# Turning an attention head's softmax weights by VectorE's blocks and a trip through DRAM in place of TensorE, in the second layer's mixer B

## The chip, the cores and the metric

One core of one Trainium2 chip runs the whole program. The metric is device time in microseconds (us), the median of three runs of the kernel before: 2664.96 us, lowest 2664.18, highest 2666.12. The names of the engines in the profile: PE is TensorE (PEld its weight loads), DVE is VectorE, ACT is ScalarE, POOL is GpSimd, SP is SyncE, which here only issues DMAs (SPq is its queue).

## The reference

The model is an encoder trunk of two layers on 256 tokens with 2048 channels. Each layer has a parallel mixer and a gated, convolved feed-forward part. Cut to what the change touches:

```python
h = rmsnorm(x, norm_mix[l]) * (1.0 + sc_a) + sh_a
qa, ka, va, qb, kb, vb, ga, gb = split_cols(h @ w_in[l])
...
ya = window_attention(qa, ka, va, sink_a[l]) @ w_proj_a[l]          # mixer A, 8 heads
...
yb = neighbourhood_attention(qb, kb, vb, rel_bias_b[l]) @ w_proj_b[l]  # mixer B, 8 heads
merged = jax.nn.sigmoid(ga) * ya + jax.nn.sigmoid(gb) * yb
x = x + gt_a * (merged @ w_out[l])
```

A head of mixer B is attention of 256 queries over 256 keys, each of 128 elements, with a learned bias and a mask on the scores: `p = softmax(q k^T * scale + bias)`, then `o = p v`. All of it is float32.

## The kernel before

**Weights.** All weight matrices are cut into 128x128 blocks and streamed from DRAM in the order in which they are used. Sixteen blocks are a unit (1 MB, tile `w`, pool `raw` with four buffers). A unit is loaded by SP (L286) and split in two halves: ScalarE copies a half into a rounded float32r part (L297) and VectorE computes the remainder (L298). Each half is a tile `hl`, of which there are four buffers, so that two units can be ready at once. A product is three matmuls a block (L314, L315, L316): high by high, high by low, low by high. The modulation weights (`aw`, L225) use the same four `raw` buffers, and VectorE reduces each of them in one long instruction (L226).

**What sets the order.** The tensor program is written out in the order of the weight stream. After each unit `Stream.tick` runs `bg.tick()`: first what was deferred to this tick, then each background job by its rate, a number of steps a tick. Attention is such a job: a step moves every live head one step on and may launch one more. In the second layer it runs at 0.4 steps a unit (`ATT[1]`) until mixer A's projection is done, and from then on, beside gate B, at `ATT_B[1]` = 0.21. Gate B has 16 units. At its end `bg.finish(job)` runs whatever steps are left, and mixer B's projection follows. Each engine works through its own queue in order; a planner that simulates the engines places instructions in these queues, so that one engine's instruction can stand ahead of its place in the program.

**A head of mixer B** (`head_b`, then `attend`) loads its bias into the tile `p` (L825) and splits q and k into halves at launch. Its steps then are:

1. scores on TensorE (L607), bias and row maximum on VectorE (L610), exponential and sums on ScalarE (L618), reciprocal on VectorE (L624), scaling on ScalarE (L626);
2. four 128x128 transposes on TensorE into one PSUM tile `tp` (L631), then the split of `tp` into `pT`, a rounded part on ScalarE (L389) and a remainder on VectorE (L390), then the split of v;
3. the product of v and `pT` on TensorE (L639) and its split into `oA` or `oB` (L641, L642).

The transposes are needed because the scores lie with queries across partitions, while the product wants keys there. `p` has two buffers, `pT` one. q and k of a pack of four heads lie in a tile (`packs[1]`, `packs[2]`); after launch their place in it is not read again.

Of the kernel before, what the change touches and what calls it, by code (L numbers as in the profile page):

```python
# [9 lines left out]
F32 = mybir.dt.float32  # L10
F32R = mybir.dt.float32r
AF = mybir.ActivationFunctionType
ALU = mybir.AluOpType
AX = mybir.AxisListType

P = 128
L = 2
D = 2048
S = 256
# [7 lines left out]
EPS = 1e-6  # L27
NEG = -1e30
SCALE = HEAD ** -0.5
GRID_W, NA_KH, NA_KW = 64, 8, 16  # L30


QKV_GROUPS = [1024, 0, 512, 2560, 3584, 1536, 3072, 4096, 2048]
# [45 lines left out]
H_RATE = [2.7, 1.7]  # L79

ATT = [1.288, 0.4]
ATT_B = [0.21, 0.21]

SCORES_3 = (1,)

ADA_ORDER = [[p * KC + k for k in range(KC) for p in ps] for ps in ((0, 1), (2,), (3, 4), (5,))]
ADA_ORDER = [i for part in ADA_ORDER for i in part]
# [47 lines left out]
def encoder(ctx: ExitStack, tc: tile.TileContext, a: dict, out: bass.AP):  # L135
    nc = tc.nc
    pool = lambda name, bufs, **kw: ctx.enter_context(tc.tile_pool(name=name, bufs=bufs, **kw))
# [12 lines left out]
    ev = pool("ev", 3)  # L150
    at = pool("at", 2)
    sm = pool("sm", 3)
    mm = pool("mm", 4, space=bass.MemoryType.PSUM)
    ax = pool("ax", 3, space=bass.MemoryType.PSUM)

    ident = const.tile([P, P], F32, name="ident")
    make_identity(nc, ident[:])
# [11 lines left out]
    def load(src, shape, name, p=const, **kw):  # L169
        t = p.tile(shape, F32, name=name, **kw)  # L170
        nc.sync.dma_start(t[:], src)
        return t
# [103 lines left out]
                pass  # L276

    bg = Paced()

    def unit_steps(l, u, by_halves=False):  # L280

        raw = rawp.tile([P, UB * P], F32, name=f"w{l}_{u}", tag="raw")
        if not by_halves:
            nc.sync.dma_start(raw[:], a["ws"][l, u])  # L286
        halves = []
        streamed = any(m == "w_in" and mo < GATE_A // P for m, _, mo in STREAMS[l][u * UB : (u + 1) * UB])
        at = OFF if streamed else 0
        for j in range(2):  # L290
            n = UB * P // 2
            hl = hlp.tile([P, 2 * n + ROW], F32R, name=f"hl{l}_{u}_{j}", tag="hl")
            hl = hl[:, at : at + 2 * n].rearrange("p (a n) -> p a n", a=2)
            r = raw[:, j * n : (j + 1) * n]
            if by_halves:
                nc.sync.dma_start(r, a["ws"][l, u][:, j * n : (j + 1) * n])
            nc.scalar.copy(hl[:, 0], r)  # L297
            nc.vector.tensor_tensor(out=hl[:, 1], in0=r, in1=hl[:, 0].bitcast(F32), op=ALU.subtract)  # L298
            halves.append(hl)
            if j == 0:  # L300
                yield halves
# [84 lines left out]
    def split(dst, src, scale=None):  # L386

        if scale is None:
            nc.scalar.copy(dst[:, 0], src)  # L389
            nc.vector.tensor_tensor(out=dst[:, 1], in0=src, in1=dst[:, 0].bitcast(F32), op=ALU.subtract)  # L390
            return
        nc.scalar.activation(out=dst[:, 0], in_=src, func=AF.Copy, scale=scale)
        nc.vector.scalar_tensor_tensor(
            out=dst[:, 1], in0=src, scalar=scale, in1=dst[:, 0].bitcast(F32), op0=ALU.mult, op1=ALU.subtract
        )
# [202 lines left out]
    def by(x):  # L598

        return ((0, 0), (0, 1), (1, 0))[: 2 * len(x) - 1]  # L600

    def attend(q, k, v, p, mask, scale, sink, o):

        sc = ax.tile([P, 2, S], F32, name="sc", tag="ax")
        for t in range(2):
            for i, j in by(q):
                nc.tensor.matmul(sc[:, t], q[i][:, t * P : (t + 1) * P], k[j], start=i + j == 0, stop=(i, j) == by(q)[-1])  # L607
        m = sm.tile([P, 2], F32, name="m", tag="m")
        for t in range(2):
            nc.vector.tensor_tensor_reduce(  # L610
                out=p[:, t], in0=sc[:, t], in1=mask[:, t], scale=scale, scalar=-3.0e38 if sink is None else sink,
                op0=ALU.add, op1=ALU.max, accum_out=m[:, t : t + 1],
            )
        nm = sm.tile([P, 2], F32, name="nm", tag="nm")
        nc.vector.tensor_scalar(out=nm[:], in0=m[:], scalar1=-1.0, scalar2=None, op0=ALU.mult)
        den = sm.tile([P, 2], F32, name="den", tag="den")
        for t in range(2):
            nc.scalar.activation(out=p[:, t], in_=p[:, t], func=AF.Exp, bias=nm[:, t : t + 1], accum_out=den[:, t : t + 1])  # L618
        if sink is not None:
            es = sm.tile([P, 2], F32, name="es", tag="es")  # L620
            nc.scalar.activation(out=es[:], in_=nm[:], func=AF.Exp, bias=sink)
            nc.vector.tensor_tensor(out=den[:], in0=den[:], in1=es[:], op=ALU.add)
        ri = sm.tile([P, 2], F32, name="ri", tag="ri")
        nc.vector.reciprocal(out=ri[:], in_=den[:])  # L624
        for t in range(2):
            nc.scalar.activation(out=p[:, t], in_=p[:, t], func=AF.Copy, scale=ri[:, t : t + 1])  # L626
        yield
        tp = ax.tile([P, 2, S], F32, name="tp", tag="ax")
        for k in range(2):
            for t in range(2):  # L630
                nc.tensor.transpose(tp[:, k, t * P : (t + 1) * P], p[:, t, k * P : (k + 1) * P], ident[:])  # L631
        pT = at.tile([P, 2, 2, S], F32R, name="pT", tag="pT", bufs=1)
        split(pT, tp[:])
        v = v()
        yield
        po = ax.tile([P, 512], F32, name="po", tag="ax")
        for i, j in by(v):
            for b in range(2):
                nc.tensor.matmul(po[:, :S], v[i][:, b], pT[:, j, b], start=i + j + b == 0, stop=i + b == 2)  # L639
        o = o()  # L640
        nc.scalar.copy(o[:, 0], po[:, :S])  # L641
        nc.vector.tensor_tensor(out=o[:, 1], in0=po[:, :S], in1=o[:, 0].bitcast(F32), op=ALU.subtract)  # L642
# [91 lines left out]
    tables = []  # L734

    def small(l):
# [7 lines left out]
        cw = load(a["cw"][l], [P, 2 * FC, 4], f"cw{l}", lay, tag="cw", bufs=1)  # L744
        nc.vector.tensor_scalar(out=gains[:, 2:3], in0=gains[:, 2:3], scalar1=SCALE, scalar2=None, op0=ALU.mult)
        rots = []
# [11 lines left out]
    for l in range(L):  # L758
# [35 lines left out]
        kTa, qTa = packs[0][:, 0:3:2], packs[0][:, 4:12]  # L794
# [3 lines left out]
        oA, oB = [], []  # L798

        def head_a(i):  # L800
            g = i // (HA // GA)
            if i >= 6:
                oA.append(paired(F32R, f"oA{l}_{i}"))
            elif i % 2 == 0:
                o = place(("y0", "y1", "y2")[i // 2], 4, F32R, f"oA{l}_{i}")
                oA.extend((o[:, :2], o[:, 2:]))
            q = in_halves(qTa[:, i], f"qA{l}_{i}", "qh", l in SCORES_3)
            if i % (HA // GA) == 0:
                kvs[0] = in_halves(kTa[:, g], f"kA{l}_{g}", "kh", l in SCORES_3)
            k = kvs[0]  # L810
            yield
            p = at.tile([P, 2, S], F32, name="p", tag="p")

            def v():
                if i % (HA // GA) == 0:
                    kvs[1] = in_halves(packs[0][:, 1:4:2, g * HEAD : (g + 1) * HEAD], f"vA{l}_{g}", "vh", True)
                return kvs[1]

            yield from attend(q, k, v, p, tables[0], SCALE, sink[:, i : i + 1], lambda: oA[i])

        def head_b(hb):
            b, i = packs[1 + hb // 4], hb % 4
            v = b[:, 4:8].rearrange("p (t a) s -> p t (a s)", t=2)
            p = at.tile([P, 2, S], F32, name="p", tag="p")
            nc.sync.dma_start(p[:], a["bias"][l, hb])  # L825
            q = in_halves(b[:, 8 + i], f"qB{l}_{hb}", "qh", l in SCORES_3)
            k = in_halves(b[:, i], f"kB{l}_{hb}", "kh", l in SCORES_3)
            yield
            yield from attend(
                q, k, lambda: in_halves(v[:, :, i * HEAD : (i + 1) * HEAD], f"vB{l}_{hb}", "vh", True), p, p, 1.0, None,  # L830
                lambda: oB_of(hb),
            )

        def oB_of(hb):
            if hb == 0:
                o = place("a", 12, F32R, f"oB{l}_{hb}")
                oB.extend(o[:, 2 * i : 2 * i + 2] for i in range(6))
            elif hb == 6:
                oB.extend(chunks_of(sp, "b0", 6, f"oB{l}_{hb}", 2))
            return oB[hb]  # L840
# [30 lines left out]
        for pi, (groups, gates) in enumerate(parts):  # L871
            last = pi == len(parts) - 1
            for g, part in enumerate(groups):
                have_h(part)
                pss = st.tokens(h, part)
                if pi == max(0, len(parts) - 2) and g == 0:
                    gains, sink, cw, rots = small(l)
                dst = packs[g // 3][:, 4 * (g % 3) : 4 * (g % 3) + 4]
                rows = dst.rearrange("p (t a) s -> p t (a s)", t=2)
# [54 lines left out]
        if l:  # L934
            bg.pace(job, ATT_B[l])
        gb = []
        for tag in ("y0", "y1", "y2"):
            t = place(tag, 4, F32, f"gb{l}_{tag}")
            gb += [t[:, i] for i in range(4)]
        for i in range(2):  # L940
            t = paired(F32, f"gb{l}_{i}")
# [56 lines left out]
        for gi, chunks in enumerate(FF_GROUPS):  # L998
# [34 lines left out]
            for cs in sets:  # L1033
                fns = [lambda p, e=e, c=c: e(p, c) for c in cs for e in (g_evac, v_evac)]
                src = bare.chunks if gi == 0 and cs[0] < BARE[1] // 2 else bare.h
# [113 lines left out]
```

## Time and profile before

| | |
|---|---|
| median of three runs | 2664.96 us (2664.18 to 2666.12) |
| span of the profiled execution, first to last instruction | 2663.2 us; the page gives no other time of that execution |
| instructions | 50845 |
| data read from DRAM, written to it | 695.03 MB, 2.10 MB |
| tile `tp`: transposes (L631) | 128, from 281.1 us to 1796.0 us, both layers and both mixers |
| second layer, attention | 1440 to 1802 us; mixer B's products (L639) from 1663.4 to 1802.2 us |
| second layer, mixer A's projection, gate B, mixer B's projection | about 1657 to 1708, 1708 to 1801, 1801 to 1847 us |

The page shows busy times and shares of the span for each engine, then the chain of work that ended last, followed back from the last instruction, then groups of instructions by source line. In a group, the numbers behind the first bar are the busy time in us and the mean of one in ns, and behind the second the idle time of that engine just before these instructions and what ended it. In a timeline, a row is the start, the duration, the engine, the line, the operation and the tiles, with a count. Matmuls are pipelined and their ends are modelled, so the start-to-start time is the one to read.

### The profile page before, as it was taken

The numbers are of one execution on the slowest core, as the hardware profiler recorded it, in microseconds if no ns is written. First come the engines' busy times: TensorE is split into PE (matmuls) and PEld (weight loads), VectorE is DVE, ScalarE is ACT, GpSimd is POOL, SyncE is SP. The second block draws the span as 40 slices with busy tenths as digits, with TensorE's granted clock in tenths as the row PEclk, the third lists the DMA queues.
The fourth block names the chain that finished last, engine by engine and source line by source line (L and its number), as shares of the span: only waits on it lengthen the run. The fifth ranks groups of instructions, "written<-read, shape, count | busy, mean of one in ns | idle before, by whom it ended". The sixth has DMA issues, their size and how long they took to land.

```text
span 2663.2 us, 50845 instructions
## 1 busy us (share of the span) xinstructions
PE 2650.9 (100%) x21256; PEld 2565.7 (96%) x21256; DVE 2102.2 (79%) x2959; ACT 1412.8 (53%) x2284; POOL 36.2 (1%) x25
## 2 busy tenths in 40 slices
PE   9999999999999999999999999999999999999999
PEld 7888899999999999999998889999999999999999
DVE  8898998997987888788976667768888866655664
ACT  5445865456644555355555566554565445544553
POOL 0001100000000000000000000000000000000000
PEclk9999999999999999999999999999999999999999
DMA  9987789885787878788766666666747765555554
GB/s 372 351 327 292 262 300 352 317 320 199 291 294 287 302 288 295 289 294 289 290 217 254 228 229 231 245 252 253 285 173 288 297 256 190 190 194 194 197 191 143
DMA packets 102039, 700.41 MB, mean 263 GB/s; under 512 B 12721, under 2 KB 15025, under 8 KB 17969
## 3 DMA queue, kind: packets, MB, share of 16 engines
q1 hardware_dynamic: 101810, 697.17, 71.4%
q8 instruction: 166, 2.72, 0.4%
q14 instruction: 63, 0.52, 0.1%
HBM read 695.03 MB, written 2.10 MB: 262 GB/s over the span
## 4 chain that ended last, share of the span: by engine, by line
PE 89%; DVE 6%; ACT 1%; issue 1%; DMA 1%; POOL 0%; SPq 0%; DVEq 0%; ACTq 0%
PE ps L314 25%; PE ps L316 25%; PE ps L315 25%; PE ps_t L377 4%; PE ps_t L379 4%; PE ps_t L378 4%; DVE hl L298 2%; DVE aw L226 2%; DMA aw<-in_aw 1%; PE sc L607 1%; PE po L639 1%; ACT hl L297 1%; PE tp L631 1%; POOL qrs L441 0%; PE qtp L580 0%
## 5 line engine op out<-in xcount | busy, mean ns | idle before, releaser
L298 DVE TENSOR_TENSOR hl<-w,hl 128x1024 fp32r<-128x1024 f32 x928 | 1128.3, 1222 | 360.0 <-ACT hl L297 357.6
L297 ACT CAST hl<-w 128x1024 fp32r<-128x1024 f32 x928 | 970.7, 1049 | 748.5 <-PE ps L316 518.1
L314 PE MATMUL ps<-h,hl 128*128 128x256 f32 x3328 | 922.8, 277 | 1.3 <-DVE ya L915 0.6
L315 PE MATMUL ps<-h,hl 128*128 128x256 f32 x3328 | 919.8, 276 | 0.0
L316 PE MATMUL ps<-h,hl 128*128 128x256 f32 x3328 | 919.8, 277 | 0.0
L314 PEld LDWEIGHTS ps<-h,hl 128*128 128x128 f32 x3328 | 624.8, 188 | 2.4 <-DVE ya L915 0.8
L315 PEld LDWEIGHTS ps<-h,hl 128*128 128x128 f32 x3328 | 625.3, 188 | 0.4 <-DVE h L470 0.2
L316 PEld LDWEIGHTS ps<-h,hl 128*128 128x128 f32 x3328 | 624.4, 188 | 0.0
L226 DVE CUSTOM_DVE_ANT_0 aw<-aw,cact,ab 128x2048 f32<-128x2048 f32 x189 | 443.5, 2347 | 48.8 <-DMA aw<-in_aw 47.8
L377 PE MATMUL ps_t<-hl,h 128*128 128x512 f32 x576 | 223.1, 392 | 2.6 <-ACT h L469 2.1
L378 PE MATMUL ps_t<-hl,h 128*128 128x512 f32 x576 | 224.9, 391 | 0.3
L379 PE MATMUL ps_t<-hl,h 128*128 128x512 f32 x576 | 224.3, 390 | 0.0
L994 DVE SCALAR_TENSOR_TENSOR u<-ps,cw,u 128x255 f32<-128x255 f32 x304 | 146.1, 481 | 66.5 <-ACT u L992 62.2
L992 ACT ACTIVATE u<-ps,cw 128x256 f32<-128x256 f32 x152 | 85.9, 565 | 187.9 <-PE ps L316 187.5
L316 PE MATMUL ps<-merged,hl 128*128 128x256 f32 x512 | 141.8, 277 | 0.4 <-DVE hl L298 0.4
L315 PE MATMUL ps<-merged,hl 128*128 128x256 f32 x512 | 141.6, 277 | 0.0
L314 PE MATMUL ps<-merged,hl 128*128 128x256 f32 x512 | 141.6, 277 | 0.0
L315 PE MATMUL ps<-act_o,hl 128*128 128x256 f32 x512 | 141.4, 276 | 0.0
L316 PE MATMUL ps<-act_o,hl 128*128 128x256 f32 x512 | 141.3, 276 | 0.0
L314 PE MATMUL ps<-act_o,hl 128*128 128x256 f32 x512 | 141.2, 276 | 0.0
L377 PEld LDWEIGHTS ps_t<-hl,h 128*128 128x128 f32 x576 | 107.9, 188 | 26.1 <-ACT h L469 3.1
L378 PEld LDWEIGHTS ps_t<-hl,h 128*128 128x128 f32 x576 | 108.1, 188 | 23.7 <-DVE hl L298 1.9
(231 smaller groups left out, 4612.5 us busy)
## 6 DMA issues: line engine op xcount, KB each, us to landing
w<-in_ws SPq DMA_DIRECT2D x463, 1024.0 KB, 4.9
aw<-in_aw SPq DMA_DIRECT2D x189, 1024.0 KB, 6.1
p<-in_bias SPq DMA_DIRECT2D x16, 256.0 KB, 4.2
x<-in_xT SPq DMA_DIRECT2D x4, 512.0 KB, 5.3
aw_o<-in_aw SPq DMA_DIRECT2D x2, 1024.0 KB, 12.3
out<-x SPq DMA_DIRECT2D x16, 128.0 KB, 2.1
w<-in_ws SPq DMA_DIRECT2D x2, 512.0 KB, 11.7
aw_b<-in_aw SPq DMA_DIRECT2D x1, 1024.0 KB, 18.1
```

Of the source, the lines that this page charges most:

```text
L226: nc.vector.tensor_tensor_reduce(out=raw[:], in0=raw[:], in1=cact[:], scale=1.0, scalar=ab[:, i : i + 1], op0=ALU.mult, op1=ALU.add, accum ...
L297: nc.scalar.copy(hl[:, 0], r)
L298: nc.vector.tensor_tensor(out=hl[:, 1], in0=r, in1=hl[:, 0].bitcast(F32), op=ALU.subtract)
L314: nc.tensor.matmul(out, hi, act[0], start=first, stop=False)
L315: nc.tensor.matmul(ps[:, :S], hi, act[1], start=False, stop=False)
L316: nc.tensor.matmul(out, lo, act[0], start=False, stop=last)
L377: nc.tensor.matmul(ps[:], xh, hi, start=kc == kcs[0], stop=False)
L378: nc.tensor.matmul(ps[:], xh, lo, start=False, stop=False)
L379: nc.tensor.matmul(ps[:], xl, hi, start=False, stop=kc == kcs[-1])
L607: nc.tensor.matmul(sc[:, t], q[i][:, t * P : (t + 1) * P], k[j], start=i + j == 0, stop=(i, j) == by(q)[-1])
L992: nc.scalar.activation(out=u, in_=ps, func=AF.Identity, scale=w[:, 1:2], bias=w[:, 3:4])
L994: nc.vector.scalar_tensor_tensor(out=u[:, to], in0=ps[:, of], scalar=w[:, j : j + 1], in1=u[:, to], op0=ALU.mult, op1=ALU.add)
```

## The change

In the second layer, all eight heads of mixer B (`MOVED[1] = (0, 8)`) no longer use TensorE's transposes. VectorE turns the two 128x256 halves of `p` in blocks of 32x32 into the room that q and k of the head occupied. For each of these, GpSimd's queue issues four DMAs of 32 KB, which carry the blocks to a DRAM tile at the place where the whole transpose wants them, in pieces of 128 bytes. SP's queue reads the two transposed halves back, 128 KB each, four ticks later (`BACK[1] = 4`), or in the head's step two steps on if that comes first. A manual dependency makes each read wait also for the newest unit's second weight split on VectorE (`halved`). `pT` is then split from these two SBUF rows, one after the other, in place of from PSUM. A head has two steps more. `ATT_B[1]` goes from 0.21 to 0.4. The first layer and mixer A keep TensorE's transposes (`MOVED` has zeros there).

```diff
-ATT_B = [0.21, 0.21]
+ATT_B = [0.21, 0.4]
...
+BACK = [3, 4]
+MOVED = [(0, 0), (0, 8)]
...
+    dram = pool("dram", 2, space=bass.MemoryType.DRAM)
...
+    def read_back(dst, src):
+
+        tc.add_manual_dep(nc.sync.dma_start(dst, src).ins, halved[0], BEHIND)
+
+    def later(n, fn):
+
+        if n == 0:
+            fn()
+        else:
+            bg.defer(lambda: later(n - 1, fn))
+
+    def turned_blocks(p, rows, n, tag):
+
+        y = dram.tile([P, n, S], F32, name=tag, tag=tag)
+        to = y[:].rearrange("(b i) n (t a j) -> t a i n b j", i=BLOCK, t=2, a=P // BLOCK)
+        for t, row in enumerate(rows):
+            nc.vector.transpose(out=row, in_=p[t])
+            src = row.rearrange("p (n b j) -> p n b j", n=n, j=BLOCK)
+            for a in range(P // BLOCK):
+                nc.gpsimd.dma_start(to[t, a], src[a * BLOCK : (a + 1) * BLOCK])
+        return y
...
-            nc.vector.tensor_tensor(out=hl[:, 1], in0=r, in1=hl[:, 0].bitcast(F32), op=ALU.subtract)
+            halved[0] = nc.vector.tensor_tensor(
+                out=hl[:, 1], in0=r, in1=hl[:, 0].bitcast(F32), op=ALU.subtract
+            ).ins.name
...
-        tp = ax.tile([P, 2, S], F32, name="tp", tag="ax")
-        for k in range(2):
-            for t in range(2):
-                nc.tensor.transpose(tp[:, k, t * P : (t + 1) * P], p[:, t, k * P : (k + 1) * P], ident[:])
-        pT = at.tile([P, 2, 2, S], F32R, name="pT", tag="pT", bufs=1)
-        split(pT, tp[:])
+        if rows is not None:
+            rows = rows()
+            y = turned_blocks([p[:, t] for t in range(2)], rows, 2, "pY")
+
+            def back():
+                for k in range(2):
+                    read_back(rows[k], y[:, k])
+
+            back = once(back)
+            later(BACK[sink is None], back)
+            yield
+            yield
+            back()
+            pT = at.tile([P, 2, 2, S], F32R, name="pT", tag="pT", bufs=1)
+            for k in range(2):
+                split(pT[:, :, k], rows[k])
+        else:
...
-                lambda: oB_of(hb),
+                lambda: oB_of(hb), (lambda: [b[:, 8 + i], b[:, i]]) if hb < MOVED[l][1] else None,
```

`once(fn)` calls `fn` the first time only.

More of the change, by code (lines that the diff above doesn't have):

```diff
@@ L29 @@
 SCALE = HEAD ** -0.5
+BEHIND = mybir.DependencyInfo(mybir.DependencyClass.Sync, mybir.DependencyReason.DATA)
 GRID_W, NA_KH, NA_KW = 64, 8, 16
+BLOCK = 32
 QKV_GROUPS = [1024, 0, 512, 2560, 3584, 1536, 3072, 4096, 2048]
@@ L278, in encoder, with once, run @@
     bg = Paced()
+    halved = [None]
+    def once(fn):
+        due = [fn]
+        def run():
+            if due:
+                due.pop()()
+        return run
+    def read_back(dst, src):
[14 more added lines that the diff above has]
+        return y
     def unit_steps(l, u, by_halves=False):
@@ L600, in by, with attend @@
         return ((0, 0), (0, 1), (1, 0))[: 2 * len(x) - 1]
-    def attend(q, k, v, p, mask, scale, sink, o):
+    def attend(q, k, v, p, mask, scale, sink, o, rows=None):
         sc = ax.tile([P, 2, S], F32, name="sc", tag="ax")
@@ L627, in attend @@
         yield
-        tp = ax.tile([P, 2, S], F32, name="tp", tag="ax")
-        for k in range(2):
-            for t in range(2):
-                nc.tensor.transpose(tp[:, k, t * P : (t + 1) * P], p[:, t, k * P : (k + 1) * P], ident[:])
-        pT = at.tile([P, 2, 2, S], F32R, name="pT", tag="pT", bufs=1)
-        split(pT, tp[:])
+        if rows is not None:
[13 more added lines that the diff above has]
+        else:
+            tp = ax.tile([P, 2, S], F32, name="tp", tag="ax")
+            for k in range(2):
+                for t in range(2):
+                    nc.tensor.transpose(tp[:, k, t * P : (t + 1) * P], p[:, t, k * P : (k + 1) * P], ident[:])
+            pT = at.tile([P, 2, 2, S], F32R, name="pT", tag="pT", bufs=1)
+            split(pT, tp[:])
         v = v()
@@ L817, in v, with rows @@
                 return kvs[1]
-            yield from attend(q, k, v, p, tables[0], SCALE, sink[:, i : i + 1], lambda: oA[i])
+            def rows():
+                spare = ev.tile([P, S], F32, name=f"spare{l}_{i}", tag="r", bufs=2)
+                return [qTa[:, i], spare[:]]
+            yield from attend(
+                q, k, v, p, tables[0], SCALE, sink[:, i : i + 1], lambda: oA[i], rows if i < MOVED[l][0] else None
+            )
         def head_b(hb):
```

## The prediction

> **What bounds the kernel now.** I read the page first: busy times, then the chain that ended last.
>
> ```profile
> span 2663.2 us, 50845 instructions
> PE 2650.9 (100%) x21256; PEld 2565.7 (96%) x21256; DVE 2102.2 (79%) x2959; ACT 1412.8 (53%) x2284; POOL 36.2 (1%) x25
> PE 89%; DVE 6%; ACT 1%; issue 1%; DMA 1%; POOL 0%; SPq 0%; DVEq 0%; ACTq 0%
> ```
>
> TensorE is busy for all but 12 us of the span and carries 89% of the chain; GpSimd is nearly empty. So the change is worth what it takes from TensorE's queue, less what it makes TensorE wait. An average can hide a stage with another limit, so I next asked for the busy time in the two stages in which mixer B of the second layer runs: the projection of mixer A (1657 to 1708 us) and gate B (1708 to 1801 us).
>
> ```profile
> core 0: us, PE busy (x) PEld busy (x) DVE busy (x) ACT busy (x) POOL busy (x), PEclk, DMA share, GB/s
> 1657.00:1708.00 51.00, 51.00 (x447) 51.00 (x446) 40.79 (x73) 27.73 (x51) 0.00 (x0) 1.00 0.69 252
> 1708.00:1801.00 93.00, 93.00 (x820) 93.00 (x819) 59.45 (x82) 48.71 (x84) 0.00 (x0) 1.00 0.67 246
> ```
>
> TensorE has no gap there, at a granted clock of 1.00. VectorE has 10 of 51 us and 34 of 93 us free, the DMA engines a third. Hence nothing can be gained here but TensorE instructions that disappear, and much can be added elsewhere before it shows. The waits of this stage say how far ahead the others are:
>
> ```profile
> L298 DVE TENSOR_TENSOR hl<-w,hl 128x1024 fp32r<-128x1024 f32 x53 | 64.7, 1224 | 44.8 <-ACT hl L297 44.8
> L297 ACT CAST hl<-w 128x1024 fp32r<-128x1024 f32 x54 | 56.7, 1050 | 45.8 <-PE ps L316 45.8
> L226 DVE CUSTOM_DVE_ANT_0 aw<-aw,cact,ab 128x2048 f32<-128x2048 f32 x9 | 21.1, 2348 | 1.0 <-DMA aw<-in_aw 0.9
> ```
>
> Groups of 1640 to 1800 us. ScalarE's weight copies wait for TensorE to free a buffer, and VectorE waits for ScalarE: both are paced by TensorE. No weight copy waits for a DMA.
>
> **What is removed: 32 transposes on TensorE.** Busy time overlaps between matmuls (each row says 0.28 us), so I take start-to-start times in TensorE's timeline.
>
> ```profile
> 1763.72 0.28 PE L316 MATMUL ps<-h,hl 128*128 128x256 f32 x1
> ...
> 1765.77 0.28 PE L316 MATMUL ps<-h,hl 128*128 128x256 f32 x1
> 1765.88 0.85 PE L639 MATMUL po<-pT,vB 128*128 128x256 f32 x6
> 1766.56 0.60 PE L631 MATMUL tp<-ident,p 128*128 128x128 f32 x4
> 1766.92 0.94 PE L607 MATMUL sc<-kB,qB 128*128 128x256 f32 x6
> 1767.70 0.28 PE L314 MATMUL ps<-h,hl 128*128 128x256 f32 x1
> ```
>
> From 1763.72 to 1765.77 lie 18 intervals (six turns of L314, L315, L316): 2.05 / 18 = 0.114 us a matmul. From 1765.77 to 1767.70 are 1.93 us with 12 wide matmuls and the closing interval in them: 13 x 0.114 = 1.48. The rest, 0.45 us, is what four transposes cost (0.11 each, not the 0.27 of a busy row).
>
> ```profile
> L631 PE MATMUL tp<-ident,p x32: 270/272/273, 1646.0 to 1796.0; 128*128 128x128 f32 x32
> L389 ACT CAST pT<-tp x8: 587/598/604, 1646.9 to 1796.7; 128x512 fp32r<-128x512 f32 x8
> L390 DVE TENSOR_TENSOR pT<-tp,pT x8: 679/681/683, 1648.3 to 1798.0; 128x512 fp32r<-128x512 f32 x8
> ```
>
> That tile's instructions from 1640 to 1800 us: 32 transposes, so eight groups of four. **8 x 0.45 = 3.6 us off TensorE.**
>
> **What the quicker pace moves.** With 0.21 steps a unit in gate B the last head isn't done when the stage ends; its last step is run there, and the first merge waits for it:
>
> ```profile
> 1804.66 0.40 PE L314 MATMUL ps<-oB,hl 128*128 128x256 f32 x2
> 1805.36 0.38 PE L315 MATMUL ps<-oB,hl 128*128 128x256 f32 x1 [0.30 <-DVE oB L642]
> ```
>
> The second of the two starts at 1804.78, the next at 1805.36: 0.58 less one interval, 0.47 us lost. At 0.4 a head needs two steps more, but 16 units give six steps (0.4 x 16 = 6.4). The head launched last, one step before the stage, needs five more steps and ends about a unit before the stage does. **0.5 us gained.** If I miscounted a step, the last read back and its splits run bare at that point: 4.2 us to land, as a bias load (row below), and 1.7 for the splits, some 6 us, once.
>
> **What is added on VectorE and ScalarE.** A head gets two block transposes of 128x256 and, in place of one split of 128x512 out of PSUM, two splits of 128x256 out of SBUF. The nearest rows are the splits of v, also 128x256 from SBUF:
>
> ```profile
> L389 ACT CAST vB<-packB 128x256 fp32r<-128x256 f32 x8 | 3.4, 421 | 0.0
> L390 DVE TENSOR_TENSOR vB<-packB,vB 128x256 fp32r<-128x256 f32 x8 | 3.3, 415 | 0.0
> ```
>
> No block transpose is in this trace. Its bounds are nothing and the 0.68 us of the 128x512 row; I take 0.42, the row with as many elements. VectorE: 2 x 0.42 + 2 x 0.42 - 0.68 = 1.0 us a head, 8 us in all; with about four heads in the projection stage it goes from 40.8 to 44.8 of 51 us. ScalarE: 2 x 0.42 - 0.60 = 0.24 us a head. On the path: nothing, hidden by the free time above. Without that cover it would be 8 us.
>
> **What is added on the queues.** GpSimd issues 8 writes of 32 KB a head, 64 in all; SP issues 16 reads of 128 KB, in the queue that also loads weights (w), modulation weights (aw) and bias. Per head 0.26 MB go out and come back, 4.2 MB in about 150 us: 28 GB/s beside 246. Hidden by the third of DMA time that is free.
>
> A read back waits for all eight writes, and what is queued behind it on SP are the loads of w and aw, on which VectorE and then TensorE wait. So its cover matters. The unit is 48 x 0.114 = 5.46 us.
>
> ```profile
> 1703.31 0.90 ACT L626 ACTIVATE p<-p,ri 128x256 f32<-128x256 f32 x2
> ```
> ```profile
> 1708.32 0.60 PE L631 MATMUL tp<-ident,p 128*128 128x128 f32 x4
> ```
>
> Head by head, p is ready at 1704.2, 4.1 us before its turn at the end of a unit, so VectorE can turn it that early. The read back also waits for the second half of the newest unit's weights:
>
> ```profile
> 1754.61 1.22 DVE L298 TENSOR_TENSOR hl<-w,hl 128x1024 fp32r<-128x1024 f32 x1
> 1758.98 1.23 DVE L298 TENSOR_TENSOR hl<-w,hl 128x1024 fp32r<-128x1024 f32 x1 [1.25 <-ACT hl L297]
> 1761.97 1.23 DVE L298 TENSOR_TENSOR hl<-w,hl 128x1024 fp32r<-128x1024 f32 x1 [1.76 <-ACT hl L297]
> ```
>
> The two halves at 1758.98 and 1761.97 belong to the unit that TensorE starts at 1767.70 and ends at 1773.2. So the second is done (1763.2) 10 us before the tick at which the read back is called. Four units: 21.8 + 4.1 - 10 = 16 us, less 0.8 for the two transposes: **15 us for eight writes.** That wait on a split costs SP nothing by itself: the next w load waits for such a split already, to get its buffer. Past those 15 us SP is held, aw and w come later, and VectorE waits. TensorE has its reserve before that: the half of 1754.61, behind an aw reduction, is ready at 1755.8 for the unit before, which starts 5.46 us ahead of the turn at 1765.88: 4.6 us. So a head costs nothing until its writes take about **19.5 us (15 + 4.5), 2.4 us each if they ran strictly one after the other.**
>
> ```profile
> w<-in_ws SPq DMA_DIRECT2D x463, 1024.0 KB, 4.9
> aw<-in_aw SPq DMA_DIRECT2D x189, 1024.0 KB, 6.1
> p<-in_bias SPq DMA_DIRECT2D x16, 256.0 KB, 4.2
> out<-x SPq DMA_DIRECT2D x16, 128.0 KB, 2.1
> ```
>
> No write in 128-byte pieces and no GpSimd DMA is in this trace. The issue itself is short on SP:
>
> ```profile
> L825 SPq DMA_DIRECT2D p<-in_bias x8: 327/328/423, 1617.9 to 1738.1; - x8
> ```
>
> Overlapped, with such an issue of 0.33 us and 2.1 us to land, eight take 7 x 0.33 + 2.1 = 4.4 us; strictly serial at 2.1 us (the only row that writes to DRAM) 16.8; serial at the 4.2 us of the bias loads 33.6. I take 2.1, since it is the write, and expect overlap: covered.
>
> [...]
>
> **The sum.** Span 2663.2 - 3.6 - 0.5 = 2659.1 us. The page shows no other time for the profiled execution; the median of the runs is 2664.96, 1.8 us above its span, and I keep that distance: 2660.9, called **2661.0 us**, 0.15% less. This kernel's measurement can tell about 0.2% (5.3 us) from no change, so the forecast itself lies within. Its own range is 2660 to 2664: the saving of 4.1 us whole, or with up to 3 us lost again to small waits.
>
> **Rivals.**
>
> Rival 1, SP held by late writes (slower). The place is the read back in SP's queue, the point 19.5 us for eight writes. At 2.7 us each, serial, 21.6 - 19.5 = 2.1 us a head, 17 us in all, less 4.1: 2678. At 4.2 us each 14.1 a head, 113 in all: 2774. For it: small pieces, a queue not yet used in this kernel, aw loads that already come just in time (0.9 us of waits above). Against: DMA engines a third free, eight writes that needn't wait for one another, and the cover above.
>
> Rival 2, GpSimd and VectorE block one another (slower). The only GpSimd work in mixer B's preparation is a tiny power:
>
> ```profile
> L441 POOL TENSOR_TENSOR qrs<-qss,mhalf 128x8 f32<-128x8 f32 (+1 forms) x14 | 30.0, 2143 | 540.3 <-DVE qss L440 540.3
> ```
> ```profile
> 1640.00:1800.00 160.00, 160.00 (x1404) 160.00 (x1403) 110.81 (x172) 86.64 (x153) 0.00 (x0) 1.00 0.66 242
> ```
>
> If each of 64 issues held both engines for 2.1 us, as one such row lasts, VectorE would lose 137 us where it has 49 of 160 us free (1640 to 1800, columns as above), 8 of which the added work takes: about 96 us late, 2757. At 0.33 us an issue it would be 21 us, inside the free time: nothing. The deciding point is 41 / 64 = 0.64 us an issue. For it only that GpSimd's rows are long; against it that the trace shows no such blocking anywhere. [...]
>
> Rival 3, nothing comes through: freed TensorE time turns into waits for VectorE, whose queue now also holds transposes. Then 2664 to 2666, the time of before. Against: 45 us of VectorE waits for ScalarE in this stage.
>
> Rival 4, the sum is short: waits around the old transposes, invisible as gaps, also go, over 5.3 us gained, 2659. Against: TensorE has no gap in the stage.
>
> **How the numbers follow.** Forecast 0.63; rival 1 0.19; rival 2 0.07; rival 3 0.04; rival 4 0.07. Forecast and rival 3 lie within 0.2% (0.67), rivals 1 and 2 are slower (0.26), rival 4 is faster (0.07). The range takes in the forecast's own, the edge of rival 4 at 2659, and rival 1 up to its milder price, 2678; beyond that lie the rest of rival 1 and rival 2, together under 0.2.
>
> **What the profile after would show.** Right: 96 transposes of tile tp in place of 128, wide matmuls at 0.114 us from po straight on to sc, no idle before the first merge, VectorE some 8 us busier, GpSimd's writes of a head done within 15 us, SP's read backs waiting for VectorE's splits alone. Wrong: read backs waiting for DMA; aw or w waits that grow from 1 us in this stage; idle TensorE between 1650 and 1810 us.

## The result and the profile after

The changed kernel takes 2660.94 us, the median of 21 runs (2659.68 to 2665.25), beside 2664.96 us before (21 runs); the ratio is 0.9985, with a 95% interval of 0.9979 to 0.9990. The profiled execution took 2661.44 us, its span 2659.3.

The page of the changed kernel, the lines that answer to those of before:

```profile
span 2659.3 us, 50973 instructions
PE 2647.6 (100%) x21224; PEld 2562.6 (96%) x21224; DVE 2106.2 (79%) x2983; ACT 1411.5 (53%) x2292; POOL 75.0 (3%) x89
```

The span is 3.9 us shorter. TensorE has 32 instructions fewer and 3.3 us less busy time, GpSimd 64 more and 39 us more. TensorE's timeline around a step that has both a product and scores (start, duration, engine, line, operation, count):

```profile
1692.24 0.28 PE L357 MATMUL ps<-oA,hl 128*128 128x256 f32 x1
1692.36 0.86 PE L697 MATMUL po<-pT,vB 128*128 128x256 f32 x6
1693.05 0.84 PE L648 MATMUL sc<-kB,qB 128*128 128x256 f32 x6
1693.73 0.28 PE L355 MATMUL ps<-oA,hl 128*128 128x256 f32 x1
```

From 1692.24 to 1693.73 are 1.49 us for 13 intervals, 0.114 each: the 0.45 us of the four transposes are gone and nothing has taken their place. The stages, in the windows of before and in the whole stretch:

```profile
core 0: us, PE busy (x) PEld busy (x) DVE busy (x) ACT busy (x) POOL busy (x), PEclk, DMA share, GB/s
1657.00:1708.00 51.00, 51.00 (x447) 51.00 (x446) 42.66 (x80) 29.23 (x54) 15.08 (x25) 1.00 0.81 283
1708.00:1801.00 93.00, 93.00 (x821) 93.00 (x820) 63.83 (x99) 50.54 (x92) 17.40 (x29) 1.00 0.76 271
1640.00:1800.00 160.00, 160.00 (x1405) 160.00 (x1405) 118.66 (x200) 89.36 (x165) 39.37 (x64) 1.00 0.77 273
```

TensorE is still without a gap, now also at the first merge. VectorE went from 110.8 to 118.7 us of 160, the DMA engines from 0.66 to 0.77. What the added parts took, and the waits of 1640 to 1810 us that touch them:

```profile
L313 DVE STREAM_TRANSPOSE packB<-p x16: 401/440/446, 1640.1 to 1742.5; 128x256 f32<-128x256 f32 x16
L316 POOL DMA_DIRECT2D pY<-packB x64: 612/612/782, 1640.9 to 1750.9; - x64
pY<-packB POOLq DMA_DIRECT2D x64, 32.0 KB, 4.2
packB<-pY SPq DMA_DIRECT2D x16, 128.0 KB, 2.7
POOL pY L316 <- issue: 44.4, 28, 4.2
SPq L299 <- DVE hl L337: 20.2, 6, 4.8
DVE aw L232 <- DMA aw<-in_aw: 4.3, 4, 1.8
ACT pT L430 <- DMA packB<-pY: 1.1, 1, 1.1
```

A block transpose takes 0.44 us, a write 0.61 to issue and 4.2 to land (median, from issue on). SP's read backs wait for VectorE, six of the eight for a weight split, and never for the writes. The waits for aw grew from 1.8 to 4.3 us in these 170 us, without a wait of TensorE. The first head, GpSimd's timeline and then SP's:

```profile
1640.91 2.00 POOL L316 DMA_DIRECT2D pY<-packB  x3 [25.36 <-DVE packB L313]
1644.42 1.83 POOL L316 DMA_DIRECT2D pY<-packB  x3 [1.52 <-issue]
1650.43 1.33 POOL L316 DMA_DIRECT2D pY<-packB  x2 [4.18 <-issue]
```
```profile
1660.70 0.81 SPq L299 DMA_DIRECT2D packB<-pY  x2
```

GpSimd stops after three writes and again after three. The eight are issued by 1651.8, and by the trace's landings the last is there at 1654.0, 13.1 us after the first was issued. The read back starts 6.7 us later. Over the eight heads the writes take 13.1 to 17.2 us from the first issue to the last landing, and the read back starts 17.3 to 24.8 us after the first issue, at the least 3.3 us after the last landing.

### The profile page after: what moved, and what is told of

Same layout as the page of the kernel before. It is cut to its first block, busy times and chain, and to the rows that moved or that the text cites. A ratio compares the mean times of both kernels' runs of the same rounds, so it can differ in the third digit from the quotient of the medians.

```text
span 2659.3 us, 50973 instructions
## 1 busy us (share of the span) xinstructions
PE 2647.6 (100%) x21224; PEld 2562.6 (96%) x21224; DVE 2106.2 (79%) x2983; ACT 1411.5 (53%) x2292; POOL 75.0 (3%) x89
## 3 DMA queue, kind: packets, MB, share of 16 engines
q0 software_dynamic: 2048, 2.10, 0.3%
## 4 chain that ended last, share of the span: by engine, by line
PE 90%; DVE 5%; DMA 2%; ACT 1%; issue 1%; POOL 0%; DVEq 0%; ACTq 0%
PE ps L355 25%; PE ps L357 25%; PE ps L356 25%; PE ps_t L420 4%; PE ps_t L418 4%; PE ps_t L419 4%; DVE hl L337 2%; DVE aw L232 1%; DMA aw<-in_aw 1%; PE sc L648 1%; PE po L697 1%; ACT hl L336 1%; PE tp L689 0%; PE qtp L621 0%; DMA w<-in_ws 0%
## 5 line engine op out<-in xcount | busy, mean ns | idle before, releaser
L337 DVE TENSOR_TENSOR hl<-w,hl 128x1024 fp32r<-128x1024 f32 x928 | 1128.4, 1222 | 338.7 <-ACT hl L336 332.1
## 6 DMA issues: line engine op xcount, KB each, us to landing
aw_o<-in_aw SPq DMA_DIRECT2D x2, 1024.0 KB, 13.1
```

Source lines behind the costliest of these rows:

```text
L337: halved[0] = nc.vector.tensor_tensor(out=hl[:, 1], in0=r, in1=hl[:, 0].bitcast(F32), op=ALU.subtract).ins.name
```

## The experiments

Each kernel was timed beside the kernel before on the same chip. Kernels are the changed one with the edit shown, if nothing else is said.

**The quicker pace alone** (an edit to the kernel before).

```diff
-ATT_B = [0.21, 0.21]
+ATT_B = [0.21, 0.4]
```

> The kernel before with the quicker pace alone (0.4 steps a unit beside gate B), all transposes still on TensorE. Theory (32 transposes at 0.114 us carry the gain, the pace takes away only the stop of 0.47 us ahead of the first merge): 2664.5 us, ratio to before 0.9998, and no TensorE wait for oB. Rival (the pace carries the gain): about 2661.

Measured: 2664.31 us, ratio 0.9998 (0.9989 to 1.0007). The profile has no TensorE wait between 1640 and 1830 us. The pace doesn't carry the gain; 0.5 us is too small for this interval to show.

**No transposes at all.**

```diff
-MOVED = [(0, 0), (0, 8)]
+MOVED = [(0, 0), (0, 0)]
+BARE_P = [False, True]
...
-        if rows is not None:
+        if bare_p:
+            pT = at.tile([P, 2, 2, S], F32R, name="pT", tag="pT", bufs=1)
+            for k in range(2):
+                split(pT[:, :, k], p[:, k])
+        elif rows is not None:
```

`BARE_P` is handed to mixer B's heads as `bare_p`.

> The changed kernel without any transpose in the second layer's mixer B: p is split as it lies, so the weights enter the product unturned; no turning, no writes, no reads back, no extra steps, pace 0.4. Theory (the whole detour is hidden): the same as the changed kernel, 2660.9 us, ratio 0.9985. Rival (the detour costs TensorE something and the saving is larger than 3.6 us): 2 us or more below, 2659 or less.

Measured: 2660.47 us, ratio 0.9982 (0.9973 to 0.9991). That is 0.5 us beside the changed kernel, inside the interval: the detour through VectorE, GpSimd, DRAM and SP costs nothing that can be told.

**TensorE's transposes left in beside the detour.**

```diff
+            tp = ax.tile([P, 2, S], F32, name="tp", tag="ax")
+            for k in range(2):
+                for t in range(2):
+                    nc.tensor.transpose(tp[:, k, t * P : (t + 1) * P], p[:, t, k * P : (k + 1) * P], ident[:])
             rows = rows()
```

> The changed kernel with TensorE's 32 transposes left in beside the detour, their result unused. Theory: they cost 3.6 us again, 2664.5 us, ratio 0.9998. Rival (the gain came from the pace or from SP no longer waiting for TensorE's transposes): stays near 2661 in the first case; in the second also about 2664.5, but with idle TensorE in the stage and not with more matmuls.

Measured: 2664.84 us, ratio 1.0000 (0.9991 to 1.0009). The gain is gone. TensorE's timeline has the groups of four again, as before the change, and no wait in the stage:

```profile
1694.44 0.60 PE L673 MATMUL tp<-ident,p 128*128 128x128 f32 x4
```

The interval of this kernel (0.9991 to 1.0009) and that of the changed kernel (0.9979 to 0.9990) don't overlap. These three runs together show that the 32 transposes on TensorE are the gain.

**The old pace with the new path.**

```diff
-ATT_B = [0.21, 0.4]
+ATT_B = [0.21, 0.21]
```

> The changed kernel at the old pace of 0.21. Theory: beside gate B there are three steps in place of six, so the last three run bare at its end, where the last head's writes (14 us), read back (3 us) and splits (1 us) stand open: TensorE waits some 10 us once, 2671 us (2666 to 2676). Rival (pace is worth only the 0.47 us): 2661.4.

Measured: 2663.56 us, ratio 0.9996 (0.9987 to 1.0005), some 3 us more than the changed kernel and not 10; the two intervals just overlap. The one new wait of TensorE, the chain of work that led to it (start, length, what), and the busy times right after it (columns as above):

```profile
PE ps L356 <- DVE oB L700: 2.6, 1, 2.6
1792.76 7.39 DMA aw<-in_aw
1800.29 0.14 DVE aw L232
1802.65 0.35 DVE oB L700
1803.60:1806.20 2.60, 2.60 (x15) 2.60 (x14) 1.74 (x4) 0.61 (x3) 0.00 (x0) 0.52 0.90 302
```

The last steps do run at the end of the gate, as expected, but TensorE has the projection of the heads that are done to work on, and its one wait is not for the last head. It is for the split of the sixth head (oB), which lies behind an aw reduction in VectorE's queue. That aw was loaded late: SP stood at the last read back until 1790.4, the last head's writes having landed at 1790.3, and issued aw at 1792.8. So this is the chain of rival 1, once, for 2.6 us where 10 were expected. TensorE then runs for 2.6 us at 0.52 of the clock, so the wait is paid, by estimate, about one and a half times. At the old pace the last read back comes too early for its writes; the quicker pace avoids that.

**The read back two units or one unit after the turn.**

```diff
-BACK = [3, 4]
+BACK = [3, 2]        # and in a second kernel [3, 1]
```

> The changed kernel with the read back two units after the turn in place of four. In the changed kernel the last write of a head starts to move 4 to 11 us ahead of its read back. Theory (cover): 10.9 us of cover go, SP is held 1 to 8 us at the read backs, TensorE's reserve of 4.5 us takes most of that, some 12 us lost over eight heads: 2672 us (2663 to 2685), with SP waiting for DMA at the read back. Rival (the wait on the split or the planner sets the place of the read back, the number of units doesn't matter): 2661.

> The changed kernel with the read back one unit after the turn. Theory (cover): 16.4 us of cover go, SP is held 7 to 14 us a head, less 4.5 us of reserve, some 50 us lost: 2711 us (2685 to 2725). Rival (the place doesn't matter): 2661.

Measured: 2667.74 us, ratio 1.0014 (1.0004 to 1.0023), and 2671.55 us, ratio 1.0025 (1.0015 to 1.0034). The waits of 1640 to 1830 us, first with two units, then with one:

```profile
SPq L299 <- DMA pY<-packB: 60.0, 22, 9.8
DVE aw L232 <- DMA aw<-in_aw: 29.9, 9, 4.9
PE ps L357 <- DVE hl L337: 2.7, 1, 2.7
```
```profile
SPq L299 <- DMA pY<-packB: 73.4, 27, 10.1
DVE aw L232 <- DMA aw<-in_aw: 32.2, 9, 6.7
PE ps L357 <- DVE hl L337: 5.5, 3, 2.9
```

The chain is the one of rival 1: SP held by the writes, aw late, VectorE late, TensorE waiting. Its price is smaller than expected, with two units by 4 us and with one unit by 39. Held for 73 us in all, 9 a head, SP made TensorE wait 5.5 us in all; after the longest of these waits TensorE ran at half the clock for 6.8 us, by estimate some 3.4 us more.

**The read back without its wait on the weight split.**

```diff
-        tc.add_manual_dep(nc.sync.dma_start(dst, src).ins, halved[0], BEHIND)
+        nc.sync.dma_start(dst, src)
```

> The changed kernel with the read back's extra wait on the newest weight split left out; it still waits for its own writes. Theory (the extra wait is what puts the read back four units on in SP's queue; without it the planner puts it where it believes the writes are done, and SP is held when they take longer): slower, about 2673 us (2663 to 2690), with SP waiting for DMA at the read back. Rival (four units of program order are enough): 2661.

Measured: 2668.69 us, ratio 1.0019 (1.0010 to 1.0028), as the theory had it.

```profile
SPq L299 <- DMA pY<-packB: 72.0, 26, 11.1
PE ps L357 <- DVE hl L337: 4.0, 2, 3.1
```

SP is held almost as long as with one unit: the place in the program alone doesn't put the read back four units on. The extra wait does.

**The writes issued by SP.**

```diff
-                nc.gpsimd.dma_start(to[t, a], src[a * BLOCK : (a + 1) * BLOCK])
+                nc.sync.dma_start(to[t, a], src[a * BLOCK : (a + 1) * BLOCK])
```

> The changed kernel with the 64 writes issued by SP in place of GpSimd. Theory (only TensorE's queue and the late loads matter; 64 issues of 0.33 us are 21 us of a queue that mostly waits): 2661 to 2663 us. Rival (SP is held at the writes, which wait for VectorE's turns, and at the read backs, and its weight loads come late): 5 us or more slower, 2666 and up.

Measured: 2677.23 us, ratio 1.0047 (1.0034 to 1.0060). The theory fell; the rival held. A head's eight issues on SP, and the waits:

```profile
1639.54 5.56 SPq L316 DMA_DIRECT2D pY<-packB  x8
SPq L316 <- DVE packB L313: 27.5, 7, 6.5
ACT hl L336 <- DMA w<-in_ws: 17.0, 8, 8.8
PE ps L355 <- ACT hl L336: 6.9, 4, 3.1
pY<-packB SPq DMA_DIRECT2D x64, 32.0 KB, 2.1
```

SP waits for VectorE's turns (27.5 us) and spends 5.6 us on a head's issues (42 us on all 64, where 21 were expected), and the weight loads behind them come late. Which engine issues the writes is worth 16 us here (2677.23 - 2660.94). How much of that is SP's waits at the writes, and how much the time of the issues themselves, this run doesn't part. The writes themselves were quicker: 2.1 us to land where GpSimd's took 4.2, and the first head's last landing seen is 6.3 us after its first issue.

**VectorE's turns four times over.**

```diff
-            nc.vector.transpose(out=row, in_=p[t])
+            for _ in range(4):
+                nc.vector.transpose(out=row, in_=p[t])
```

> The changed kernel with each block transpose on VectorE done four times in place of once: 48 more, some 20 us of VectorE work in the stage. Theory (VectorE's added work is hidden; it is free for about 41 of 160 us in the changed kernel): 2661 us, ratio 0.9985, at most 1 us more. Rival (the detour's VectorE work shows): a good part of 20 us, 2670 or more.

Measured: 2661.29 us, ratio 0.9986 (0.9977 to 0.9995). The stretch of 1640 to 1800 us:

```profile
1640.00:1800.00 160.00, 160.00 (x1405) 160.00 (x1404) 132.04 (x246) 89.31 (x164) 39.36 (x64) 1.00 0.78 273
```

VectorE works 13 us more there than in the changed kernel and TensorE has no gap: VectorE's part is hidden with room to spare.

**Mixer A of the second layer too.**

```diff
-ATT = [1.288, 0.4]
+ATT = [1.288, 0.45]
...
-MOVED = [(0, 0), (0, 8)]
+MOVED = [(0, 0), (8, 8)]
```

> The changed kernel with mixer A's eight heads of the second layer moved too, read back three units after the turn, and the second layer's pace before gate B at 0.45 in place of 0.4, so that their two extra steps fit ahead of mixer A's projection. Theory (each four transposes off TensorE are 0.45 us where the cover lasts; DMA engines and VectorE are a third free in that stage too): 2660.9 - 3.6 = 2657.3 us, ratio 0.9971. Rival (three units don't cover the writes of about 14 us, or the last head runs bare): 2661 or more.

Measured: 2663.83 us (2660.25 to 2668.76), ratio 0.9995 (0.9986 to 1.0003): no better than the changed kernel. The profiled execution is the fastest of the eleven, so what the others lost more isn't in it. In it SP is held at read backs for 40 us, and TensorE has one new wait. That wait, and rows of GpSimd, VectorE and ScalarE ahead of it:

```profile
PE sc L648 <- ACT packB L622: 2.1, 1, 2.1
1539.62 1.67 POOL L482 TENSOR_TENSOR qrs<-qss,mhalf 128x8 f32<-128x8 f32 x1
1549.00 2.35 DVE L232 CUSTOM_DVE_ANT_0 aw<-aw,cact,ab 128x2048 f32<-128x2048 f32 x1 [1.36 <-DMA aw<-in_aw]
1551.53 0.91 ACT L667 ACTIVATE p<-p,ri 128x256 f32<-128x256 f32 x2 [3.17 <-DVE ri L665]
1555.82 1.27 ACT L622 ACTIVATE packB<-qtp,gains 128x512 f32<-128x512 f32 x2
```

VectorE stands 1.4 us for aw and reduces it before the reciprocal of a head (L665); ScalarE stands 3.2 us for that reciprocal, and the turned q and k (L622), for which TensorE waits, come behind the weight copies that ScalarE then has to do. In that stage GpSimd also computes the power for the norms of q and k (L482), between the writes of a head, but it was done at 1541.3, 14 us before L622. That the late aw is the cause is argued from these rows; no run took it away.

**The first layer's mixer B too.**

```diff
-MOVED = [(0, 0), (0, 8)]
+MOVED = [(0, 8), (0, 8)]
```

> The changed kernel with the first layer's mixer B moved too. There the DMA engines are busy for 0.85 to 0.93 of the time and VectorE for 57 of 60 and 87 of 100 us in the stages that would hide it, against 0.69 and 41 of 51 in the second layer. Theory (the saving is whole only under cover): the 3.6 us are lost again to late loads and more, 2663 us (2660 to 2675), with SP held at the read backs and TensorE waiting between 340 and 500 us. Rival (DMA and VectorE load don't matter as long as the read back comes four units later): 2657.3.

Measured: 2678.26 us, ratio 1.0045 (1.0029 to 1.0060), dearer than the range that I gave. The page's whole span:

```profile
ACT hl L336 <- DMA w<-in_ws: 67.3, 24, 13.1
SPq L299 <- DMA pY<-packB: 31.5, 15, 7.3
PE ps L357 <- DVE hl L337: 8.6, 10, 2.8
PE ps L355 <- ACT hl L336: 7.1, 4, 4.7
```

The same row of the changed kernel:

```profile
ACT hl L336 <- DMA w<-in_ws: 38.8, 18, 4.4
```

The detour in the first layer cost 17 us beside the changed kernel (2678.26 - 2660.94), against the 3.6 us that it takes off TensorE. Two things act there, and this run doesn't part them. Ahead of gate B attention runs there at 1.288 steps a unit (`ATT[0]`), so by the program a head's two steps are over in under two units and the read back is called then, not after four: the first three heads are read back 11.8 to 14.0 us after their first write, in the moment in which the last one lands, and SP is held for 22.8 us. TensorE waits 8.4 us from 340 to 395 us. From 395 to 500 us the read backs come late enough and SP isn't held, but weight loads are: ScalarE waits 41 us for them, in the changed kernel 11, with the DMA engines busy for 0.91 of the time, and TensorE waits 6.0 us. After these waits the granted clock was half for 17 us in all. The rival, which says that the load doesn't matter if the read back comes four units later, was thus put to the test by the later heads alone, and there weight loads came late all the same.

**Half the DMA scratch** (`dynamic_dma_scratch_size`).

```diff
-    nc = _bacc.Bacc("TRN2", target_bir_lowering=False, num_devices=1, dynamic_dma_scratch_size=1024)
+    nc = _bacc.Bacc("TRN2", target_bir_lowering=False, num_devices=1, dynamic_dma_scratch_size=512)
```

> [...] In the changed kernel GpSimd stops for 44 us in all between the writes of a head, mostly after three. Theory (these stops are a wait for room in that scratch, and set how long eight writes take): more stops, after one or two writes, a head's writes take half as long again, SP is held at read backs, 2664 to 2675. Rival (the stops have another cause): the same stops and 2661.

Measured: 2737.02 us, ratio 1.0270 (1.0256 to 1.0284). GpSimd's first writes, and the waits of the whole span:

```profile
1642.15 0.79 POOL L316 DMA_DIRECT2D pY<-packB  x1 [25.35 <-DVE packB L313]
1645.38 0.63 POOL L316 DMA_DIRECT2D pY<-packB  x1 [2.44 <-issue]
pY<-packB POOLq DMA_DIRECT2D x64, 32.0 KB, 1.9
SPq L299 <- DMA pY<-packB: 134.0, 32, 15.9
PE ps L357 <- DVE hl L337: 49.3, 10, 15.1
```

It stops after every write, and issues the next 0.3 us after the last has landed. So the size sets the stops, as the theory had it: up to three writes are issued in a row with 1024, one with 512. (In the changed kernel at most three are under way at a time, and each of the 28 stops ends 0.1 to 0.3 us after a landing; eight stops follow three writes, the others one or two.) The time is far above the range that I gave: a head's writes now take 21 to 29 us, SP is held for 17 us a head, and TensorE waits 49 us for VectorE. A write that is alone in the queue lands in 1.9 us (median). A larger size was not tried.

## Why the prediction was right

The time (2661.0 forecast, 2660.94 measured), the sign and the mechanism came out as forecast: TensorE's 32 transposes go and the detour is hidden. Three sizes behind "hidden" were off, one against the forecast and two in its favour, and that they came out covered is in part luck.

- **Transposes, 3.6 us:** right, and shown by the runs with and without them. Start-to-start times gave it; the busy rows would have given 32 x 0.27 = 8.7.
- **The first merge, 0.5 us:** the wait is gone from the profile, with the pace alone too; the time is too small to be shown by itself.
- **VectorE and ScalarE, hidden:** right. 0.44 us a turn where I took 0.42, 7.9 us more VectorE work where I summed 8.
- **The writes:** wrong in size. I took 2.1 us for one to land and expected overlap, 4.4 us for the eight of a head; they took 13.1 to 17.2 us. The 2.1 us were right for writes issued by SP (2.1) and for one at a time in GpSimd's queue (1.9). That this queue has at most three writes under way (with 1024 of scratch) was not in the working at all, nor that each then takes 4.2 us to land. Why 4.2 and not 2.1 stays open. My sign of being right, done within 15 us, failed for two heads (15.6 and 17.2).
- **The cover, 15 us:** too small. The eight heads have 17.3 to 24.8 us between first write and read back; for the first (1640.9 to 1660.7) it is 19.8 us, since p was ready earlier and the split later than in the heads that I took. With my own cover two heads would have held SP, by up to 2.2 us, still below the 19.5 us at which I saw the first cost.
- **The reserve, 4.5 us:** too small. I counted only how far VectorE's splits run ahead of TensorE. But by the sum of its rows SP waits for 173 of the 190 us from 1640 to 1830 in the changed kernel already, and for 170 in the one-unit kernel, 73 of them at the read backs: most of the hold takes the place of waits that were there anyway. (This is argued from the sums; no run shows it alone.) That is why rival 1 is real (two units, one unit, no extra wait) but cost 7 to 11 us where I priced it at 17 and more, and why my expectations of 2672 and 2711 were high.
- **A sign of being wrong that came:** I had put down waits for aw that grow from 1 us. They grew to 2.4 us in the 160 us that I had read (1640 to 1800), and TensorE waited for nothing. The sign was too strict.
- **Rival 2:** no sign of it. VectorE's splits take 1222 ns a piece (1224 before), beside 39 us of GpSimd issues from 1640 to 1800 us. An issue takes 0.61 us (median) with VectorE busy for 118.7 of these 160 us, and each of the 28 stops between issues ended 0.1 to 0.3 us after a landing.
- **Rivals 3 and 4:** out; nothing came back as a wait, and nothing beyond the sum was gained.

## What to carry to other kernels

On a full engine, cost an instruction by start-to-start times (0.114 us a matmul here, where a busy row says 0.28). A detour pays if every queue on it has room in that very stage: the same edit gained 4 us here and lost 17 in the first layer, where the DMA engines were busy (0.91 of the time) and the first read backs came early. A late consumer needs something that holds it late: its place in the program did not do it alone (2668.69 us), a wait on work of that time did (2660.94). Put a DMA that waits into a queue in which nothing urgent stands behind it (SP's in place of GpSimd's cost 16 us), and count how many that queue takes in a row (three here, one with half the scratch).

## What the runs showed of the hardware that I had not expected

GpSimd's queue took at most three of these DMAs in a row (32 packets of 1 KB each, by the trace's 2048 for 64 writes; 128-byte pieces on the DRAM side, by the program) into 1024 of scratch and one into 512, and then stood still for up to 4.2 and 5.6 us. Issuing such a write took 0.61 us (median) on either queue, GpSimd's or SP's, where a bias load took 0.33.

From about the end of a single TensorE wait of 2.1 us (mixer A too), 2.6 us (old pace), 2.7 us (two units), 2.9 us (one unit) or 3.1 us (no extra wait) the granted clock was half for 3.4 us, in the one-unit kernel for 6.8. After the one-unit kernel's wait of 1.6 us it was not. But in the kernel with the first layer's mixer B two waits of 0.9 and 0.8 us, with half a microsecond of work between them, were enough, so the length of one wait isn't all that counts. Windows of the one-unit kernel after the waits of 2.9 and of 1.6 us, then of the first-layer kernel after the two short ones:

```profile
1722.20:1728.20 6.00, 6.00 (x28) 6.00 (x29) 3.37 (x4) 0.95 (x2) 1.80 (x3) 0.50 0.99 336
1767.10:1769.50 2.40, 2.40 (x22) 2.40 (x23) 2.40 (x6) 0.00 (x0) 0.00 (x0) 1.00 0.71 174
473.80:477.10 3.30, 3.30 (x18) 3.30 (x17) 3.30 (x6) 1.75 (x2) 0.00 (x0) 0.50 1.03 392
```
